# The exponentials stay in the scores' PSUM bank, and the row sums are taken in two parts

## The chip, the core and the metric

The kernel runs on one core of a Trainium2 chip. The metric is the time of one execution in microseconds (us), as the device counts it; less is better. TensorE (PE) multiplies matrices into PSUM, a memory of eight banks of 128 partitions x 512 fp32 values each. VectorE (DVE) and ScalarE (ACT) read and write PSUM and SBUF; GpSimd (POOL) works on SBUF alone here. SyncE (SP) issues the DMAs. Each engine takes its instructions strictly in the order in which they stand in its own queue, and waits on semaphores where it needs another engine's result.

## What is computed

One layer of a bidirectional encoder, on two batches: 256 positions (the prompt) and 2048 positions (the sample), both 1024 wide.

```python
def encoder_layer(x, ...):
    h = rms_norm(x, norm_mix_g)
    q, k, v, x_br, y_br = jnp.split(h @ w_in, splits, axis=-1)
    q, k = rms_norm(q, q_norm_g), rms_norm(k, k_norm_g)   # 8 query heads, 2 key/value heads of 64
    attn = bidir_gqa(apply_axial_rope(q, tables), apply_axial_rope(k, tables), v)
    rec = recurrent_group(x_br, y_br, ...)                # convolution, two gated linear scans
    x = x + jnp.concatenate([attn, rec], axis=-1) @ w_out
    h = rms_norm(x, norm_mlp_g)
    return x + jnp.square(jax.nn.relu(h @ w_up)) @ w_down # 4096 wide

def bidir_gqa(q, k, v):        # per head, no mask
    p = jax.nn.softmax(q @ k.T / 8, axis=-1)
    return p @ v
```

The change touches the softmax and its product with v for the 2048 sample positions.

## The kernel before

**Precision.** Every matmul operand is split into a high part (rounded to the matmul's input type, fp32r, by a copy on ACT) and a low part (the exact value minus the high part, a subtraction on DVE or POOL). A product `w x` is then `wh xh + wh xl + wl xh` (`mm3`, L201 to L204). So nearly every result passes through a cast and a subtraction.

**Stages.** Stage 1 (to about 590 us) projects both batches, normalizes q and k, runs the convolutions and the forward scans, and writes q, k and v as high and low parts to device memory. Stage 2 (L804 on) runs three things beside each other, by generators that are advanced in turn (`tick`): the attention of the sample, in 32 units; the backward scans (`lru_back`, L1157); and the out-projection and MLP of one segment after another (`mlp`, L1091): first the prompt, 256 columns wide, then four segments `s0` to `s3` of 512 columns. A segment of the sample can start only when its eight attention units are done (L1188). `faster(attention(), 5)` gives attention six steps for every five of the MLP. The final order on each engine's queue is set by the recording layer, which schedules with its own model of time; it is fixed when the program is built.

**One attention unit** is one key/value head and 512 queries, so that 8 units make a segment. `guard` (L853) first computes, for the next unit, 16 products of 512 queries with 512 keys (`s_mx`, L867), each reduced on DVE to a maximum (`mx`, L868); the negative maximum becomes a 65th row of the low query operand `ql`. `values` (L956) then walks over 16 chunks of 128 keys. For each chunk:

- L963, L964, PE: two matmuls put the scores less the maximum into a PSUM bank `s` (tag `s`, two banks in pool `pss`).
- L971, ACT: `pf` = exp of the bank, into SBUF (three buffers). From here the bank is free.
- L973, ACT: `ph` = high part of `pf` (three buffers).
- L975, DVE: `pl` = `pf` - `ph`, the low part (three buffers).
- L979 (L977 for the second chunk), POOL: `acc` += `pf`, the running sum that gives the softmax's denominator.
- L967, L968, PE, three chunks later (`LAG`): the value stationary `vv`, 128 columns that hold v's high part and v's low part (64 each), times `ph` and times `pl`, both into the one bank `po`.

`combine` (L904) ends a unit: ACT copies one half of `po` (`sh`, L913), DVE adds the other half to it (`osb`, L914), `acc` is split (L917, L919). After every second unit `finish` (L880) sums `acc` over the partitions by four matmuls into `pden`, takes four reciprocals from it on DVE (L888), multiplies on POOL and stores the result.

**The MLP's PSUM.** The out-projection (`ps_o`), the up-projection (`ps_u`) and the down-projection (`ps_d`) take their banks in turn from `m0`, `m1`, `m2` (L805, `mm_tile`). A tile of `ps_u` is 24 matmuls, one of `ps_d` 12; two `ps_o` tiles are filled together by 48. They are emptied by ACT (L1021, up), by DVE (L1136, `y` += `ps_d`, down) and by DVE (L1003, out-projection). The other banks of stage 2 are two for `s`, two for `aux` (`s_mx`, `pden` and other small uses) and one for `po`: eight in all.

**Others on the engines' queues.** ACT casts the weights (L168); their low parts are taken on DVE or POOL (`wl`, L177), for the prompt's segment two thirds on POOL. DVE makes the MLP's low parts (`ul`, L1025; `h2l`, L1005), and the scans.

Of the kernel before, what the change touches and what calls it, by code (L numbers as in the profile page):

```python
# [12 lines left out]
F32 = mybir.dt.float32  # L13
FR = mybir.dt.float32r
AF = mybir.ActivationFunctionType
ALU = mybir.AluOpType
# [3 lines left out]
P = 128  # L20
D = 1024
KC = D // P
SEQ = 256
DEC = 2048
T = SEQ + DEC
NT = 512
# [25 lines left out]
def f32(ap):  # L52
    return ap.bitcast(F32)
# [23 lines left out]
def trunk(ctx, tc, xT, w_in, w_out, w_up, w_down, vecs, wa, wx, cos, sin, outT):  # L77
    nc = tc.nc
    mm = nc.tensor.matmul
    act = nc.scalar.activation  # L80
    tt = nc.vector.tensor_tensor
    stt = nc.vector.scalar_tensor_tensor
    ts = nc.vector.tensor_scalar
    gtt = nc.gpsimd.tensor_tensor
# [4 lines left out]
    def loadr(out, src):  # L89

        load(f32(out), src)
# [28 lines left out]
    v_d = {r: dtile([P, n // P, 2, P], f"v_d{r}") for r, n in (("p", SEQ), ("s", DEC))}  # L120
# [101 lines left out]
    srcs, saved, scratch = [], [], {}  # L222
    for key in keys:
# [9 lines left out]
        if first:  # L233
# [14 lines left out]
    for i in range(2):  # L248
        o = ctile([P, P], f"ones_{i}", FR)
# [22 lines left out]
    with ExitStack() as c1:  # L272
# [210 lines left out]
        def do_v(r, t0, n, ps):  # L483
            v = sl.tile([P, NT], F32, tag="gy", name="v", bufs=2)
            evac(v[:, :n], ps[:, :n])
            yield
            pt = ps_g.tile([P, NT], F32, tag="g", name="pt")
            for i in range(n // P):
                nc.tensor.transpose(pt[:, i * P:(i + 1) * P], v[:, i * P:(i + 1) * P], ident)
            yield  # L490
            p4 = pt.rearrange("p (i f) -> p i f", f=P)
            for o in range(0, n // P, 2):
                vt = sl.tile([P, NT], FR, tag="xh", name="vt", bufs=2)
                vv = vt.rearrange("p (i k f) -> p i k f", i=2, k=2)
                for kv in range(2):
                    src = p4[:, o:o + 2, 64 * kv:64 * kv + 64]
                    hi = vv[:, :, kv, 64 * kv:64 * kv + 64]
                    act(hi, src, AF.Copy)
                    tt(vv[:, :, kv, 64 - 64 * kv:128 - 64 * kv], src, f32(hi), op=ALU.subtract)
                store(v_d[r][:, t0 // P + o:t0 // P + o + 2], f32(vv))  # L500
                yield

# [299 lines left out]


    with ExitStack() as c2:  # L804
        banks[0] = itertools.cycle(("m0", "m1", "m2"))  # L805
        sm = c2.enter_context(tc.tile_pool(name="m2", bufs=1))
        kvp = c2.enter_context(tc.tile_pool(name="kv", bufs=1))
        qp = c2.enter_context(tc.tile_pool(name="q2", bufs=2))
# [3 lines left out]
        ps_x = c2.enter_context(tc.tile_pool(name="psx", bufs=1, space=PSUM))  # L812

        kv_s = [kvp.tile([P, 2, DEC], FR, tag="k1", name="k1"), kvp.tile([65, 2, DEC], FR, tag="k2", name="k2"),
                kvp.tile([P, DEC // P, 2, P], FR, tag="vv", name="vv2")]
        nc.gpsimd.memset(f32(kv_s[1][64:65]), 1.0)

        def load_kv():
            for o in range(0, DEC, NT):
                load_keys("s", *kv_s[:2], o, NT)  # L820
                yield
            for o in range(0, DEC // P, 4):
                loadr(kv_s[2][:, o:o + 4], v_d["s"][:, o:o + 4])
                yield


# [53 lines left out]
        def finish(u, accs, o_sb):  # L880
# [20 lines left out]
        finals = []  # L901
        pair = []

        def combine(u, po, acc):  # L904
            kv = units[u][2]
            rows = slice(64 * kv, 64 * kv + 64)
            other = slice(64 - 64 * kv, 128 - 64 * kv)
            if kv == 0:
                pair[:] = [sb.tile([P, NT], F32, tag="osb", name="osb", bufs=1), []]
            o_sb, accs = pair  # L910

            sh = sb.tile([P, NT], F32, tag="sh", name="sh", bufs=1)
            act(sh[rows, :], po[other, :], AF.Copy)  # L913
            tt(o_sb[rows, :], po[rows, :], sh[rows, :], op=ALU.add)  # L914
            yield
            ah = sb.tile([P, NT], FR, tag="dh", name="dh", bufs=2)
            act(ah, acc, AF.Copy)  # L917
            al = sb.tile([P, NT], FR, tag="dl", name="dl", bufs=2)
            tt(al, acc, f32(ah), op=ALU.subtract)  # L919
            accs += [(half[kv], ah), (half[kv], al)]  # L920
            yield
            if kv == 1:
                yield from finish(u, accs, o_sb)

        LAG = 3

        def attention():

            tail = []
            qt[0] = load_q(0)  # L930
            yield from guard(0)
            yield
            for u, (kvt, nk, kv, _, _, _) in enumerate(units):
                nkc = nk // P
                k1, k2, vv = kvt
# [4 lines left out]
                tail.append(values(u, po, acc, vv, kv, nkc, qd, ql, k1, k2))  # L940
                i = 0
                while i < nkc or g is not None:
                    i += 1
                    if g is not None and next(g, tail) is tail:
                        g = None
                    for v in list(tail):
                        if next(v, tail) is tail:
                            tail.remove(v)
                    yield
            while tail:  # L950
                for v in list(tail):
                    if next(v, tail) is tail:
                        tail.remove(v)
                yield

        def values(u, po, acc, vv, kv, nkc, qd, ql, k1, k2):  # L956
            p = {}
            pf0 = None
            for c in range(nkc + LAG):
                if c < nkc:  # L960
                    ks = slice(c * P, (c + 1) * P)
                    s = ps_s.tile([P, NT], F32, tag="s", name="s_t")
                    mm(s, k1[:, kv, ks], qd, start=True, stop=False)  # L963
                    mm(s, k2[:, kv, ks], ql, start=False, stop=True)  # L964
                if c >= LAG:
                    ph, pl = p.pop(c - LAG)
                    mm(po, vv[:, c - LAG, kv, :], ph, start=c == LAG, stop=False)  # L967
                    mm(po, vv[:, c - LAG, kv, :], pl, start=False, stop=c == nkc + LAG - 1)  # L968
                if c < nkc:
                    pf = pp.tile([P, NT], F32, tag="pf", name="pf", bufs=3)  # L970
                    act(pf, s, AF.Exp)  # L971
                    ph = pp.tile([P, NT], FR, tag="ph", name="ph", bufs=LAG)
                    act(ph, pf, AF.Copy)  # L973
                    pl = pp.tile([P, NT], FR, tag="pl", name="pl", bufs=LAG)
                    tt(pl, pf, f32(ph), op=ALU.subtract)  # L975
                    if c == 1:
                        gtt(acc, pf0, pf, op=ALU.add)  # L977
                    elif c > 1:
                        gtt(acc, acc, pf, op=ALU.add)  # L979
                    pf0 = pf  # L980
                    p[c] = (ph, pl)
                yield
            yield from combine(u, po, acc)

        def mean_sq(acc, n):
            ps = ps_x.tile([P, NT], F32, tag="aux", name="ps_st", bufs=2)
# [184 lines left out]


        for m in range(KC):
            ws.kept[len(srcs) - KC + m] = [t.rearrange("p a n -> p (a n)" if t is kv_s[0] else "p c a n -> p (c a n)")
                                           [:, NT * m:NT * m + NT] for t in kv_s[::2]]
        spawn(load_kv())
        spawn(faster(attention(), EVERY))
        with ExitStack() as c3:
# [95 lines left out]
```

## Time and profile before

| | |
|---|---|
| runs | 3220.81 us median of three (3219.06 to 3222.16) |
| the profiled execution | 3214.51 us, of which the span from first to last instruction is 3212.4 us |
| PE busy | 3007.6 us (94%) |
| DVE busy | 2066.8 us (64%) |
| ACT busy | 1717.7 us (53%) |
| POOL busy | 1540.9 us (48%) |
| TensorE's granted clock, mean | 0.972 of full speed |

A row of the profile's table of groups, `L975 DVE TENSOR_TENSOR pl<-pf,ph ... x512 | 612.8, 1207 | 168.9 <-ACT ph L973 161.3`, reads: line 975, on DVE, writes `pl` from `pf` and `ph`, 512 times, 612.8 us in all, 1207 ns each; DVE stood idle 168.9 us just before them, of which 161.3 us ended when ACT's `ph` came. A matmul's duration contains its passage through the array, during which the next one already runs; the distance between the starts of two is what a matmul costs.

### The profile page before, as it was taken

How to read it: one execution, taken by the hardware profiler on the slowest of the kernel's cores; microseconds unless marked ns; L12 is line 12 of the kernel's file. 1: busy time of each engine (PE TensorE's matmuls, PEld its weight loads, DVE VectorE, ACT ScalarE, POOL GpSimd, SP SyncE). 2: the span in 40 equal slices, each digit the busy share in tenths (PEclk: the TensorE clock that was granted, in tenths of full speed). 3: DMA queues.
4: the chain of work that ended last, by engine and by line, in shares of the span. 5: the costliest groups of instructions: out<-in, count | busy, mean ns of one | idle time of the engine just before them, and what ended most of it. 6: DMA issues, size and time to landing. Idle time of an engine off the chain costs nothing.

```text
span 3212.4 us, 41900 instructions
## 1 busy us (share of the span) xinstructions
PE 3007.6 (94%) x13646; PEld 2426.9 (76%) x13646; DVE 2066.8 (64%) x2554; ACT 1717.7 (53%) x2956; POOL 1540.9 (48%) x1116
## 2 busy tenths in 40 slices
PE   6699999777899999999999999999999999999998
PEld 5577677556788778888888888888778888778887
DVE  8878876699989986676667766676675311131114
ACT  5475666545566666555556655555566333343334
POOL 4446633567889964453448444443664111321104
PEclk8799999788999999999999999999999999999999
DMA  7656555887665664444447644444664655775554
GB/s 248 209 176 227 159 187 175 258 257 230 197 219 184 222 200 130 140 135 138 142 138 241 196 139 132 146 138 136 206 219 147 193 189 186 254 252 187 189 188 150
DMA packets 342395, 598.97 MB, mean 186 GB/s; under 512 B 44064, under 2 KB 72992, under 8 KB 342176
## 3 DMA queue, kind: packets, MB, share of 16 engines
q1 hardware_dynamic: 342176, 596.30, 57.6%
q8 instruction: 107, 1.75, 0.2%
q14 instruction: 112, 0.92, 0.1%
HBM read 474.52 MB, written 121.63 MB: 186 GB/s over the span
## 4 chain that ended last, share of the span: by engine, by line
PE 64%; DVE 9%; DMA 5%; issue 3%; POOL 3%; ACT 2%; SPq 1%; DVEq 0%; POOLq 0%; ACTq 0%
PE ps_u L204 8%; PE ps_u L202 8%; PE ps_u L203 8%; PE ps_d L204 7%; PE ps_d L203 7%; PE ps_d L202 7%; PE s_t L964 3%; PE s_mx L867 3%; PE s_t L963 3%; PE po L968 3%; PE po L967 3%; DVE pl L975 2%; POOL acc L979 1%; DVE mx L868 1%; PE ps_o L202 1%
## 5 line engine op out<-in xcount | busy, mean ns | idle before, releaser
L168 ACT CAST wh<-wf 128x512 fp32r<-128x512 f32 x712 | 440.3, 619 | 815.1 <-PE ps_d L203 357.2
L979 POOL TENSOR_TENSOR acc<-acc,pf 128x512 f32<-128x512 f32 x448 | 653.3, 1458 | 421.5 <-ACT pf L971 405.3
L975 DVE TENSOR_TENSOR pl<-pf,ph 128x512 fp32r<-128x512 f32 x512 | 612.8, 1207 | 168.9 <-ACT ph L973 161.3
L204 PE MATMUL ps_u<-h2h,wl 128*128 128x512 f32 (+1 forms) x1280 | 480.4, 376 | 9.8 <-POOL wl L177 3.6
L202 PE MATMUL ps_u<-h2h,wh 128*128 128x512 f32 (+1 forms) x1280 | 479.4, 375 | 3.8 <-ACT wh L168 2.0
L203 PE MATMUL ps_u<-h2l,wh 128*128 128x512 f32 (+1 forms) x1280 | 479.3, 375 | 0.7 <-DVE h2l L1005 0.7
L204 PE MATMUL ps_d<-uh,wl 128*128 128x512 f32 (+1 forms) x1248 | 463.7, 374 | 5.3 <-DVE wl L177 4.2
L202 PE MATMUL ps_d<-uh,wh 128*128 128x512 f32 (+1 forms) x1248 | 463.6, 374 | 3.1 <-ACT wh L168 2.2
L203 PE MATMUL ps_d<-ul,wh 128*128 128x512 f32 (+1 forms) x1248 | 463.3, 373 | 0.6 <-DVE ul L1025 0.5
L1023 POOL TENSOR_TENSOR rl<-rl 128x512 f32<-128x512 f32 (+1 forms) x160 | 174.5, 1091 | 601.3 <-ACT uh L1022 590.9
L868 DVE TENSOR_REDUCE mx<-s_mx 128x1 f32<-128x512 f32 x512 | 345.6, 682 | 155.2 <-PE s_mx L867 151.4
L971 ACT ACTIVATE pf<-s_t 128x512 f32<-128x512 f32 x512 | 300.4, 594 | 216.2 <-PE s_t L964 124.1
L1025 DVE TENSOR_TENSOR ul<-rl,uh 128x512 fp32r<-128x512 f32 (+1 forms) x160 | 140.2, 876 | 333.0 <-POOL rl L1023 332.8
L973 ACT ACTIVATE ph<-pf 128x512 fp32r<-128x512 f32 x512 | 317.1, 631 | 11.1 <-PE po L967 2.0
L1136 DVE TENSOR_TENSOR y<-y,ps_d 128x512 f32<-128x512 f32 (+1 forms) x272 | 170.0, 627 | 234.5 <-PE ps_d L204 234.3
L204 PEld LDWEIGHTS ps_u<-h2h,wl 128*128 128x128 f32 x1280 | 243.3, 190 | 62.6 <-POOL wl L177 5.5
L202 PEld LDWEIGHTS ps_u<-h2h,wh 128*128 128x128 f32 x1280 | 243.7, 190 | 53.6 <-ACT wh L168 2.8
L203 PEld LDWEIGHTS ps_u<-h2l,wh 128*128 128x128 f32 x1280 | 243.8, 190 | 49.7 <-DVE h2l L1005 1.1
L204 PEld LDWEIGHTS ps_d<-uh,wl 128*128 128x128 f32 x1248 | 236.7, 190 | 54.9 <-DVE wl L177 6.0
L202 PEld LDWEIGHTS ps_d<-uh,wh 128*128 128x128 f32 x1248 | 236.7, 190 | 52.6 <-ACT wh L168 3.7
L203 PEld LDWEIGHTS ps_d<-ul,wh 128*128 128x128 f32 x1248 | 236.9, 190 | 48.2 <-DVE ul L1025 1.2
L202 PE MATMUL ps_in<-hh,wh 128*128 128x512 f32 (+1 forms) x560 | 221.3, 397 | 40.7 <-DVE wh L168 18.0
(277 smaller groups left out, 5682.3 us busy)
## 6 DMA issues: line engine op xcount, KB each, us to landing
wl<-wl_d SPq DMA_DIRECT2D x624, 256.0 KB, 2.7
wf<-in_w_up_dram SPq DMA_DIRECT2D x320, 256.0 KB, 3.0
wf<-in_w_down_dram SPq DMA_DIRECT2D x320, 256.0 KB, 2.9
wl_d<-wl SPq DMA_DIRECT2D x172, 256.0 KB, 2.9
wf<-in_w_out_dram SPq DMA_DIRECT2D x80, 256.0 KB, 4.0
wh<-wh_d SPq DMA_DIRECT2D x56, 256.0 KB, 3.4
x<-in_xT_dram SPq DMA_DIRECT2D x32, 256.0 KB, 4.9
qd<-q_ds SPq DMA_DIRECT2D x64, 128.0 KB, 3.2
```

The costliest lines, as they stand in the source:

```text
L168: self.copy(i)(tile_, self.f[i])
L202: mm(ps, wh, xh, start=first, stop=False)
L203: mm(ps, wh, xl, start=False, stop=False)
L204: mm(ps, wl, xh, start=False, stop=last)
L868: nc.vector.tensor_reduce(mx[:, i, b:b + 1], s[:, :w], axis=AX.X, op=ALU.max)
L971: act(pf, s, AF.Exp)
L973: act(ph, pf, AF.Copy)
L975: tt(pl, pf, f32(ph), op=ALU.subtract)
L979: gtt(acc, acc, pf, op=ALU.add)
L1023: gtt(e[:, :n], e[:, :n], e[:, :n], op=ALU.mult)
L1025: tt(ul[:, f, :n], e[:, :n], f32(uh[:, f, :n]), op=ALU.subtract)
L1136: tt(y[:, :n], y[:, :n], ps[:, :n], op=ALU.add)
```

## The change

Six edits that belong together:

1. `values`: the exponential is written back into the scores' own bank (`act(s, s, AF.Exp)`); `pf` and its three buffers are gone. `ph` is made from the bank, `pl` is the bank less `ph`. The bank is held until `pl` is done. `ph` has four buffers instead of three.
2. `acc` on POOL sums `ph`, the high parts, instead of the full exponentials.
3. The value stationary in SBUF is 320 columns for each chunk of keys: v's low and high part of head 0, 64 columns of ones, v's high and low part of head 1. `ph` is multiplied with the 128 columns of a head into `po`, as before. `pl` is multiplied with the 128 columns that hold the high part and the ones, into a bank of its own, `pq`: half of `pq` is then the values' sum, the other half the sum of the low parts over the keys, in every partition.
4. `pq` takes the bank `m2` of stage 2; the MLP's tiles take turns on `m0` and `m1` alone.
5. `combine` and `finish`: one copy (`sd`) of `pq`'s sums on ACT and one more addition (`osb` += half of `pq`) on DVE for each unit, and one addition of `pden` and `sd` on DVE for every two units; the reciprocals then read SBUF.
6. `do_v` writes v's two parts in exchanged halves; `load_kv` loads v in eight DMAs of 512-byte pieces instead of four, and POOL fills the ones once.

```diff
@@ do_v
-                    hi = vv[:, :, kv, 64 * kv:64 * kv + 64]
+                    hi = vv[:, :, kv, 64 - 64 * kv:128 - 64 * kv]
@@ stage 2
-        banks[0] = itertools.cycle(("m0", "m1", "m2"))
+        banks[0] = itertools.cycle(("m0", "m1"))
-                kvp.tile([P, DEC // P, 2, P], FR, tag="vv", name="vv2")]
+                kvp.tile([P, DEC // P, 320], FR, tag="vv", name="vv2")]
+        nc.gpsimd.memset(f32(kv_s[2][:, :, 128:192]), 1.0)
@@ load_kv
-                loadr(kv_s[2][:, o:o + 4], v_d["s"][:, o:o + 4])
+                for kv in range(2):
+                    loadr(kv_s[2][:, o:o + 4, 192 * kv:192 * kv + P], v_d["s"][:, o:o + 4, kv])
@@ finish
+            tt(rc, pden, sd, op=ALU.add)
+            yield
             for i in range(4):
-                nc.vector.reciprocal(rc[:, i * P:(i + 1) * P], pden[:, i * P:(i + 1) * P])
+                nc.vector.reciprocal(rc[:, i * P:(i + 1) * P], rc[:, i * P:(i + 1) * P])
@@ combine
             act(sh[rows, :], po[other, :], AF.Copy)
+            act(sd[rows, :], pq[other, :], AF.Copy)
             tt(o_sb[rows, :], po[rows, :], sh[rows, :], op=ALU.add)
+            tt(o_sb[rows, :], pq[rows, :], o_sb[rows, :], op=ALU.add)
@@ attention
                 po = ps_x.tile([P, NT], F32, tag="o", name="po")
+                pq = ps_m.tile([P, NT], F32, tag="m2", name="pq")
@@ values
-                    mm(po, vv[:, c - LAG, kv, :], ph, start=c == LAG, stop=False)
-                    mm(po, vv[:, c - LAG, kv, :], pl, start=False, stop=c == nkc + LAG - 1)
+                    mm(po, vv[:, i, whole:whole + P], ph, start=i == 0, stop=i == nkc - 1)
+                    mm(pq, vv[:, i, part:part + P], pl, start=i == 0, stop=i == nkc - 1)
                 if c < nkc:
-                    pf = pp.tile([P, NT], F32, tag="pf", name="pf", bufs=3)
-                    act(pf, s, AF.Exp)
-                    ph = pp.tile([P, NT], FR, tag="ph", name="ph", bufs=LAG)
-                    act(ph, pf, AF.Copy)
+                    act(s, s, AF.Exp)
+                    ph = pp.tile([P, NT], FR, tag="ph", name="ph", bufs=LAG + 1)
+                    act(ph, s, AF.Copy)
                     pl = pp.tile([P, NT], FR, tag="pl", name="pl", bufs=LAG)
-                    tt(pl, pf, f32(ph), op=ALU.subtract)
+                    tt(pl, s, f32(ph), op=ALU.subtract)
-                        gtt(acc, acc, pf, op=ALU.add)
+                        gtt(acc, acc, f32(ph), op=ALU.add)
```

**Where the order changes.** The first place is PE's queue at the end of the prompt's MLP, where the segment `s0` must wait for its eighth attention unit. `ps_d` is the prompt's last down-projection, `ps_o` the first of `s0`. Before:

```order
L204 MATMUL ps_d<-uh,wl_11037 128x256
L967 MATMUL po<-ph,vv_5227 128x512
L867 MATMUL s_mx<-k_5225,qd 128x512
L968 MATMUL po<-pl,vv_5227 128x512
L867 MATMUL s_mx<-k_5225,qd 128x512 x4
L963 MATMUL s_t<-qd,k_5225 128x512
L964 MATMUL s_t<-ql_10216,k_5226 128x512
L877 MATMUL pm<-ident,m_11267 1x128 x4
L867 MATMUL s_mx<-k_5225,qd 128x512
L202 MATMUL ps_o<-cat_11516,wh_11072 128x512
```

One chunk's score pair stands between the two. After, the same place begins so:

```order
L204 MATMUL ps_d<-uh,wl_10939 128x256
L870 MATMUL s_mx<-k_5225,qd 128x512
L979 MATMUL po<-ph,vv_5227 128x512
L974 MATMUL s_t<-qd,k_5225 128x512
L975 MATMUL s_t<-ql_9545,k_5226 128x512
L980 MATMUL pq<-pl,vv_5227 128x512
L870 MATMUL s_mx<-k_5225,qd 128x512
L979 MATMUL po<-ph,vv_5227 128x512
```

This pattern goes on for 16 score pairs before the first `ps_o` of `s0`, with no MLP matmul among them. 136 pairs stood ahead of the prompt's last down-projection before, and 123 after; 137 and 139 stand ahead of the first `ps_o` of `s0`.

The second place is DVE's queue at the end of an attention unit inside the prompt's MLP. Before:

```order
L975 TENSOR_TENSOR pl<-pf,ph 128x512
L919 TENSOR_TENSOR dl<-acc_9021,dh 128x512
L1025 TENSOR_TENSOR ul<-rl_9578,uh 128x256
L177 TENSOR_TENSOR wl_9636<-wf_9582,wh_9634 128x512
L868 TENSOR_REDUCE mx<-s_mx 128x1
L914 TENSOR_TENSOR osb<-po,sh 64x512
```

After:

```order
L871 TENSOR_REDUCE mx<-s_mx 128x1
L922 TENSOR_TENSOR osb<-po,sh 64x512
L177 TENSOR_TENSOR wl_9107<-wf_9068,wh_9105 128x512
L1146 TENSOR_TENSOR y_5864<-y_5864,ps_d 128x256
L986 TENSOR_TENSOR pl<-s_t,ph 128x512
L923 TENSOR_TENSOR osb<-pq,osb 64x512
```

The subtraction `pl` now reads the scores' bank `s_t`, and the unit's end has a second addition, three instructions behind the first.

## Rows read from the trace of the kernel before

**Rows 1.** The page: busy tenths of the span's 40 slices.

```profile
PE   6699999777899999999999999999999999999998
...
DVE  8878876699989986676667766676675311131114
```

**Rows 2.** Busy time by stretch: window, length, each engine's busy us (instructions), clock, DMA share.

```profile
590.00:1190.00 600.00, 512.88 (x2765) 421.87 (x2766) 552.50 (x635) 352.77 (x657) 477.78 (x338) 0.94 0.69 221
1190.00:2505.00 1315.00, 1311.32 (x5669) 1053.48 (x5668) 898.78 (x1059) 761.28 (x1314) 651.49 (x473) 1.00 0.49 158
2505.00:3212.40 707.40, 688.26 (x3028) 555.29 (x3026) 162.69 (x246) 248.60 (x424) 131.11 (x117) 0.99 0.62 199
```

**Rows 3.** Groups of instructions, 590 to 1190 us, DVE: count, busy us, mean ns.

```profile
L975 DVE TENSOR_TENSOR pl<-pf,ph 128x512 fp32r<-128x512 f32 x162 | 201.9, 1259 | 12.4 <-ACT ph L973 12.4
...
L914 DVE TENSOR_TENSOR osb<-po,sh 64x512 f32<-64x512 f32 x10 | 6.8, 685 | 2.6 <-ACT sh L913 2.5
```

**Rows 4.** Groups by shape, 1190 to 2505 us, DVE: an addition that reads PSUM.

```profile
L1136 DVE TENSOR_TENSOR y<-y,ps_d 128x512 f32<-128x512 f32 x116 | 79.0, 681 | 49.4 <-PE ps_d L204 49.2
```

**Rows 5.** Groups of instructions, 590 to 1190 us, POOL.

```profile
L979 POOL TENSOR_TENSOR acc<-acc,pf 128x512 f32<-128x512 f32 x140 | 221.0, 1578 | 14.9 <-ACT pf L971 11.4
```

**Rows 6.** Groups of instructions, 590 to 1190 us, ACT.

```profile
L973 ACT ACTIVATE ph<-pf 128x512 fp32r<-128x512 f32 x162 | 100.0, 630 | 3.6 <-PE po L967 1.2
...
L971 ACT ACTIVATE pf<-s_t 128x512 f32<-128x512 f32 x162 | 94.3, 592 | 63.6 <-DVE pl L975 20.5 <-PE s_t L964 19.4 <-POOL acc L979 14.9
```

**Rows 7.** Groups by shape, 590 to 1190 us, PE: one of six alike, one of three.

```profile
L204 PE MATMUL ps_u<-h2h,wl 128*128 128x256 f32 x256 | 75.5, 297 | 6.7 <-POOL wl L177 3.6 <-DVE wl L177 3.1
...
L202 PE MATMUL ps_o<-cat,wh 128*128 128x256 f32 x44 | 14.7, 334 | 8.2 <-ACT wh L168 8.2
```

**Rows 8.** Who PE waited for, 590 to 1190 us: total us, times, longest.

```profile
PE po L968 <- DVE pl L975: 33.4, 30, 3.5
```

**Rows 9.** Timeline: start us, duration us, engine, line: one `pl` beside which POOL rested.

```profile
648.84 0.68 DVE L975 TENSOR_TENSOR pl<-pf,ph 128x512 fp32r<-128x512 f32 x1
```

**Rows 10.** Timeline from 1504 us: one chunk, and the bank's next use but one.

```profile
1504.26 0.40 PE L963 MATMUL s_t<-qd,k 128*128 128x512 f32 x1
...
1504.50 0.39 PE L964 MATMUL s_t<-ql,k 65*128 65x512 f32 x1
...
1504.98 0.60 ACT L971 ACTIVATE pf<-s_t 128x512 f32<-128x512 f32 x1 [0.36 <-DVE y L1136]
...
1506.68 1.16 DVE L975 TENSOR_TENSOR pl<-pf,ph 128x512 fp32r<-128x512 f32 x1
...
1509.83 0.39 PE L963 MATMUL s_t<-qd,k 128*128 128x512 f32 x1
```

**Rows 11.** Timeline from 1052 us: one chunk inside the prompt's MLP.

```profile
1052.06 0.39 PE L963 MATMUL s_t<-qd,k 128*128 128x512 f32 x1
...
1055.17 1.14 ACT L973 ACTIVATE ph<-pf 128x512 fp32r<-128x512 f32 x2
```

**Rows 12.** Timeline of DVE from 1056 us: the low part of that chunk.

```profile
1056.79 2.90 DVE L975 TENSOR_TENSOR pl<-pf,ph 128x512 fp32r<-128x512 f32 x2
```

**Rows 13.** Timeline of PE at 859 us: first matmul of the third `ps_d` tile.

```profile
859.57 0.28 PE L202 MATMUL ps_d<-uh,wh 128*128 128x256 f32 x1
```

**Rows 14.** Timeline of DVE at 863 us: the three `ps_d` tiles are added.

```profile
863.25 1.07 DVE L1136 TENSOR_TENSOR y<-y,ps_d 128x256 f32<-128x256 f32 x3
```

**Rows 15.** Timeline of PE at 2368 us: first matmul of one `ps_o` tile.

```profile
2368.18 0.40 PE L202 MATMUL ps_o<-cat,wh 128*128 128x512 f32 x1
```

**Rows 16.** Timeline of DVE to 2375 us: what stood ahead of a `ps_o` tile's addition.

```profile
2368.45 6.15 DVE L1046 SCALAR_TENSOR_TENSOR y<-y,gfin,r 128x512 f32<-128x512 f32 x6
2374.52 0.67 DVE L1003 TENSOR_TENSOR xr<-xr,ps_o 128x512 f32<-128x512 f32 x1
```

**Rows 17.** Busy time by stretch: the start of stage 2, and the prompt's MLP.

```profile
590.00:610.00 20.00, 14.61 (x62) 11.63 (x62) 14.82 (x19) 8.78 (x12) 10.78 (x5) 0.68 1.00 330
...
700.00:1100.00 400.00, 347.95 (x2053) 294.24 (x2053) 384.00 (x437) 244.09 (x462) 342.22 (x239) 0.96 0.64 203
```

More of the change, by code (lines that the diff above doesn't have):

```diff
@@ L878, in guard, with finish @@
             act(ql[64:65, :], pm[0:1, :], AF.Copy, scale=-1.0)
-        def finish(u, accs, o_sb):
+        def finish(u, accs, o_sb, sd):
             _, _, _, _, out, nj = units[u]
@@ L902, in trunk, with combine @@
         pair = []
-        def combine(u, po, acc):
+        def combine(u, po, pq, acc):
             kv = units[u][2]
@@ L908, in combine @@
             if kv == 0:
-                pair[:] = [sb.tile([P, NT], F32, tag="osb", name="osb", bufs=1), []]
-            o_sb, accs = pair
+                pair[:] = [sb.tile([P, NT], F32, tag="osb", name="osb", bufs=1),
+                           sb.tile([P, NT], F32, tag="sd", name="sd", bufs=1), []]
+            o_sb, sd, accs = pair
             sh = sb.tile([P, NT], F32, tag="sh", name="sh", bufs=1)
             act(sh[rows, :], po[other, :], AF.Copy)
+            act(sd[rows, :], pq[other, :], AF.Copy)
             tt(o_sb[rows, :], po[rows, :], sh[rows, :], op=ALU.add)
+            tt(o_sb[rows, :], pq[rows, :], o_sb[rows, :], op=ALU.add)
             yield
@@ L922, in combine @@
             if kv == 1:
-                yield from finish(u, accs, o_sb)
+                yield from finish(u, accs, o_sb, sd)
         LAG = 3
@@ L939, in attention @@
                 po = ps_x.tile([P, NT], F32, tag="o", name="po")
-                tail.append(values(u, po, acc, vv, kv, nkc, qd, ql, k1, k2))
+                pq = ps_m.tile([P, NT], F32, tag="m2", name="pq")
+                tail.append(values(u, po, pq, acc, vv, kv, nkc, qd, ql, k1, k2))
                 i = 0
@@ L954, in attention, with values @@
                 yield
-        def values(u, po, acc, vv, kv, nkc, qd, ql, k1, k2):
+        def values(u, po, pq, acc, vv, kv, nkc, qd, ql, k1, k2):
             p = {}
-            pf0 = None
+            whole, part = 192 * kv, 64 + 64 * kv
             for c in range(nkc + LAG):
@@ L965, in values @@
                 if c >= LAG:
-                    ph, pl = p.pop(c - LAG)
-                    mm(po, vv[:, c - LAG, kv, :], ph, start=c == LAG, stop=False)
-                    mm(po, vv[:, c - LAG, kv, :], pl, start=False, stop=c == nkc + LAG - 1)
+                    i = c - LAG
+                    ph, pl = p.pop(i)
+                    mm(po, vv[:, i, whole:whole + P], ph, start=i == 0, stop=i == nkc - 1)
+                    mm(pq, vv[:, i, part:part + P], pl, start=i == 0, stop=i == nkc - 1)
                 if c < nkc:
-                    pf = pp.tile([P, NT], F32, tag="pf", name="pf", bufs=3)
-                    act(pf, s, AF.Exp)
-                    ph = pp.tile([P, NT], FR, tag="ph", name="ph", bufs=LAG)
-                    act(ph, pf, AF.Copy)
+                    act(s, s, AF.Exp)
+                    ph = pp.tile([P, NT], FR, tag="ph", name="ph", bufs=LAG + 1)
+                    act(ph, s, AF.Copy)
                     pl = pp.tile([P, NT], FR, tag="pl", name="pl", bufs=LAG)
-                    tt(pl, pf, f32(ph), op=ALU.subtract)
+                    tt(pl, s, f32(ph), op=ALU.subtract)
                     if c == 1:
-                        gtt(acc, pf0, pf, op=ALU.add)
+                        gtt(acc, f32(p[0][0]), f32(ph), op=ALU.add)
                     elif c > 1:
-                        gtt(acc, acc, pf, op=ALU.add)
-                    pf0 = pf
+                        gtt(acc, acc, f32(ph), op=ALU.add)
                     p[c] = (ph, pl)
                 yield
-            yield from combine(u, po, acc)
+            yield from combine(u, po, pq, acc)
         def mean_sq(acc, n):
@@ L1173, in trunk @@
         for m in range(KC):
-            ws.kept[len(srcs) - KC + m] = [t.rearrange("p a n -> p (a n)" if t is kv_s[0] else "p c a n -> p (c a n)")
-                                           [:, NT * m:NT * m + NT] for t in kv_s[::2]]
+            ws.kept[len(srcs) - KC + m] = [t.rearrange("p a n -> p (a n)")[:, NT * m:NT * m + NT] for t in kv_s[::2]]
         spawn(load_kv())
```

2 lines of the change are left out of this document (1 added, 1 removed).

## The prediction

> **What bounds the kernel now.** I read the page's slices first, to see where PE has room at all [rows 1]: PE stands at nine tenths from the twelfth slice on, and at seven and eight in the four before it (562 to 883 us), while DVE stands at nine from the ninth to the fourteenth but for one slice. Then I cut the span into stretches and compare each engine's busy time with the length [rows 2]. From 1190 to 2505 us PE is busy 1311 of 1315 us, so no faster VectorE can shorten that part; after 2505 us there is no attention left, and PE has 688 of 707. What can be won lies between 590 and 1190 us, where the prompt's MLP, ten attention units and the backward scans run together. There DVE is busy 552.5 of 600 us, in the 400 us in the middle even 384 [rows 17]. PE's 512.9 us are deceptive, since a matmul's duration contains its passage. In the saturated stretch 5669 matmuls, nearly all 512 wide, take 1315 us, or 0.232 us each [rows 2]. Of the 2765 matmuls between 590 and 1190 us, 6 x 256 + 3 x 44 = 1668 are 256 wide [rows 7], which I take at half, 0.116 us; the other 1097 at most at 0.232. That is at most 448 us of need, so PE loses some 150 us there, and the row of waits names DVE's `pl` first, 33.4 us directly [rows 8]; the rest is spread over weights and tiles that also come late from a full DVE or POOL. POOL has 478 us of 600, ACT 353.
>
> The costliest DVE group there is the low part `pl`: 162 of 1259 ns [rows 3]. The same subtraction took 0.68 us where POOL rested [rows 9]. So what makes it long is POOL beside it, with which it shares something when both of its operands lie in SBUF.
>
> **The change part by part.** Sums go against the profiled execution (3214.5 us, 6.3 us or 0.2% under the median of the runs); I add the 6.3 at the end.
>
> *The subtraction from PSUM.* `pl` takes its first operand from the bank instead of from SBUF. The trace has this kind of operation: `y` += `ps_d`, 512 wide, one operand in PSUM and one in SBUF, took 681 ns on the mean of 116 [rows 4], and `osb`, half of `po` plus an SBUF operand, 685 ns inside the disturbed stretch itself, where POOL is 80% busy [rows 3, 2]. So one operand in PSUM keeps POOL out, and I take 0.681: 162 x (1.259 - 0.681) = -94 us of DVE's work. The bounds are 1.259 (nothing won) and 0.68, and the two rows stand at the lower end. The saturated stretch gets its `pl` shorter too, for nothing: PE is full there.
>
> Those rows show no price for PSUM as such: 0.681 from PSUM, 0.68 from SBUF without POOL. The Trainium skill, "Perfetto Trace Analysis", section "Optimizing Scalar/DVE Operations", states an access overhead of about 60 ns for VectorE on SBUF and 125 ns on PSUM. By that, `pl` would take about 0.745 us, an estimate from that page, and the saving would be 83 us instead of 94; the sum goes by the rows.
>
> *What DVE gets in addition.* A second `osb` for each of ten units, 10 x 0.685 = 6.9, and the addition of `pden` and `sd` for five pairs, 5 x 0.68 = 3.4. DVE's need: 552.5 - 94 + 10 = 469. If the 47 us in which it rests stay, the stretch is 517 us long: **-83 us**. This is close to the others: PE 448, POOL 478 if its operations stay as long as they are. They should get shorter when DVE's `pl` no longer meets them (`acc` takes 1578 ns now [rows 5]), but no row says by how much, and I count nothing for it. In the middle 400 us POOL has 342 and DVE would have about 384 - 62 + 7 = 329 [rows 17]: there POOL is next.
>
> *ACT.* The exponential into PSUM, and the copy `ph` out of PSUM instead of SBUF, are two operations as before, between 0.59 and 0.63 us each whichever of the two rows I take [rows 6]; one more copy `sd` per unit. ACT rests 247 us of the 600: nothing.
>
> *The ones, v's loads.* The ones cost PE no matmul: the `pl` product had 128 columns before and has now. The fill runs once on POOL, which is 10.8 us busy in the first 20 [rows 17]: nothing. v's parts (2048 x 256 x 4 bytes, 2.1 MB) come in pieces half as long, at a time when the DMA engines are 100% busy with 330 GB/s [rows 17], 6.4 us of transfer. Half the rate would cost 6.4 more, the same rate nothing; other loads stand beside, and I take **+2**. `do_v` only exchanges halves: nothing.
>
> *The scores' banks.* A bank is now held until `pl` has read it. In the saturated stretch one chunk ran from 1504.26 to 1506.68 + 1.16 = 1507.84, 3.6 us, and the bank was wanted again at 1509.83 [rows 10]: 2 us to spare, more with a shorter `pl`. In the prompt's MLP another ran from 1052.06 through a late `ph` at 1055.17 [rows 11] to the first of two `pl` that together ran from 1056.79 for 2.90 [rows 12], so to about 1058.2: 6.2 us. Two banks then allow one chunk per 3.1 us; the stretch needs one per 600 / 162 = 3.7 now and per 3.2 if it lasts 517. It just holds; that it doesn't is a rival.
>
> *The stretch of attention alone.* In the new order 16 score pairs stand ahead of `s0`'s first out-projection without an MLP matmul among them. A chunk there is five matmuls, 1.16 us, while the round of two banks is (3.6 - 0.5 for the shorter `pl`) / 2 = 1.55: 16 x 0.39 = **+6** (0 to 10, with the old life).
>
> *Two banks for the MLP.* At 859.57 the third `ps_d` tile began [rows 13]; the first of the three was only added from 863.25 on, three in 1.07 us [rows 14], so until about 863.6. With two banks PE would have waited 4 us in the old order. About eight such groups stand in the prompt's MLP, 32 us at most. But the order is made anew with two banks, and DVE has more air: between 0 and 32 I take half, **+16**. In the samples' segments tiles have 2.8 us and more of matmuls between them, and DVE's addition 0.68: nothing, but for the out-projection. At 2368.18 a `ps_o` tile began [rows 15], while the one two before it had to wait behind six final scalings of 6.15 us and was added at 2374.52 + 0.67 [rows 16]: 7 us. For the three other segments nothing to 7 each; I take 2 together: **+9** (0 to 28).
>
> *The unit's end.* `pq` is one bank; the next unit's first product into it waits for `sd` and the second `osb`, which stands three DVE instructions behind the first. Who waits would be PE, with all behind it. Three instructions of 0.68 are 2.1 us for each of ten units; the product comes three chunks, some 10 us, after the unit's last score, so mostly hidden: of 0 to 20 I take **+5**.
>
> Sum: -83 + 2 + 6 + 16 + 9 + 5 = **-45**: 3169.5 profiled, 3175.8 against the median; I say **3175**.
>
> **Rivals.**
>
> *The two MLP banks eat it.* All groups wait as in the old order: -83 + 2 + 6 + 32 + 28 + 5 = -10, or 3211. For it: `ps_d` tiles of 12 short matmuls come every 1.4 us when PE is alone, and DVE empties them in bunches. Against: DVE falls from 92% to 90% of a shorter stretch, and empties are ordered with the two banks in mind. The Trainium skill, "Perfetto Trace Analysis", section "Optimizing Tensor Performance", bears on this: it advises that independent matmul groups rotate through different PSUM banks, so that one is emptied while the next is filled; here a rotation of three becomes one of two. The row of 859.57 agrees that three are in use.
>
> *More is won.* DVE's idle time shrinks too, because POOL's operations shorten and `pl` no longer queues: DVE 469 plus 20 idle, -111, with some 10 of give-backs: -101, or 3120. For it: PE's need is only 448. Against: POOL at 478.
>
> *The score banks' round binds (slower).* Exp, copy and subtraction are done by two in-order engines that are full of other work; the bank's life includes all of that queueing. Above a life of 2 x 3.7 = 7.4 us the round sets the time, whatever DVE saves: at 8 us, 4.0 us a chunk, 162 x 0.3 = +49, or 3270. Between 6.4 and 7.4 it takes part of the gain: 6.9 would leave 41 of it. For it: the 6.2 us of one chunk. Against: that chunk's `pl` were long ones, and in the rest the exponential came sooner.
>
> *It doesn't do what it says.* `pl` stays at 1.259 us since the bank is also written by ACT, or by other causes: +10 of new DVE work and the +38 of give-backs, 3269. Against: `osb` at 685 ns in the same stretch.
>
> **How the numbers follow.** Forecast 0.59, two MLP banks 0.14, more won 0.14, score banks 0.09, not as said 0.04. The range from 3118 to 3224 takes in the forecast with its bounds, the first rival and the centre of the second, and leaves out half of the latter and both slower ones, 0.20. A measurement here can tell about 0.2% (6.4 us) from no change. Faster: 0.57 of the forecast, 0.14, and half of the first rival, 0.78. Same: 0.02 + 0.06 = 0.08. Slower: 0.09 + 0.04 + 0.01 = 0.14.
>
> **What will show it.** Right: `pl` near 0.68 us everywhere; the start of `s0`'s first out-projection some 60 us earlier; DVE's busy time in the same work down by some 80; the stretch until attention's end still with PE full; PE's waits for `pl` gone, new ones on `ps_d` or `ps_u` for DVE's additions, a few us each. Wrong: score matmuls (L974) waiting for `pl` by tens of us (score banks); MLP matmuls waiting for `y` or `ul` by over 40 us (MLP banks); `pl` over 0.9 us; or a POOL that is full from 700 to 1100 us while DVE rests.

## The result: 17.6 us faster, where 45.8 were forecast

The changed kernel takes 3203.25 us (median of five, 3193.44 to 3204.86), beside 3220.81 us for the kernel before (3218.58 to 3224.41). The ratio is 0.9939, with a 95% interval of 0.9922 to 0.9956. A second measurement, told below, gave 0.9934. So the direction of the forecast was right, and the size was two and a half times too large. The profiled execution has a span of 3203.1 us, 9.3 less than that of before (3212.4); the medians differ by more, so the places below account for the 9.3 and not for all of the 17.6.

Busy time by stretch of the changed kernel, in the columns of [rows 2]: window, length, then PE, weight loads, DVE, ACT and POOL in us (instructions), PE's granted clock, DMA share, GB/s.

```profile
590.00:1190.00 600.00, 528.98 (x2851) 438.66 (x2852) 474.13 (x670) 367.83 (x687) 431.48 (x343) 0.92 0.72 228
1190.00:2505.00 1315.00, 1311.44 (x5669) 1054.27 (x5668) 738.47 (x1077) 757.36 (x1329) 595.85 (x469) 1.00 0.50 158
```

DVE's work fell as the sum had it: 552.5 us between 590 and 1190 us before [rows 2], 474.1 now, 469 forecast. PE's matmuls in the same 600 us rose from 2765 only to 2851. The stretch to 2505 us was full before and is full now, with 160 us of DVE's work gone from it for nothing, as forecast.

The groups of that stretch, 590 to 1190 us, with count, busy us and mean ns, in the changed kernel: DVE's `pl` and the new additions, POOL's `acc`, ACT's two passes.

```profile
L986 DVE TENSOR_TENSOR pl<-s_t,ph 128x512 fp32r<-128x512 f32 x163 | 110.3, 681 | 52.3 <-ACT ph L984 51.8
...
L923 DVE TENSOR_TENSOR osb<-pq,osb 64x512 f32<-64x512 f32 x10 | 6.8, 684 | 1.3 <-ACT sd L921 1.1
...
L890 DVE TENSOR_TENSOR rc<-pden,sd 128x512 f32<-128x512 f32 x5 | 3.4, 683 | 0.0
...
L990 POOL TENSOR_TENSOR acc<-acc,ph 128x512 f32<-128x512 f32 x141 | 194.2, 1378 | 58.7 <-ACT ph L984 55.8 <-DMA r_ds<-rh 1.0
...
L984 ACT ACTIVATE ph<-s_t 128x512 fp32r<-128x512 f32 x164 | 97.1, 596 | 7.8 <-POOL acc L990 2.0
L982 ACT ACTIVATE s_t<-s_t 128x512 f32<-128x512 f32 x164 | 95.3, 583 | 57.8 <-PE s_t L975 55.7 <-DVE mx L871 0.9
```

`pl` went from 1259 [rows 3] to 681 ns, to the nanosecond what the row of `y` had promised. But where DVE stood idle 12.4 us before it, it now stands 52.3 us, waiting for ACT's `ph`: the engine that was the bound now waits.

Who PE waited for in the same stretch: us, times, longest.

```profile
PE s_mx L870 <- DVE mx L871: 21.0, 18, 2.7
PE s_t L974 <- DVE pl L986: 12.4, 11, 2.7
PE po L979 <- ACT ph L984: 11.4, 13, 3.0
```

Of the 33.4 us for `pl` at the product [rows 8], 1.3 are left. In their place stand 12.4 us in which the scores' matmul waits for the bank that `pl` still reads, 11.4 us for `ph`, and 21 for the maxima (18.2 before, in the same view).

The first 610 us from 590 us on, in three parts, before and then changed, in the columns above.

```profile
590.00:800.00 210.00, 158.50 (x733) 122.50 (x734) 195.99 (x218) 106.97 (x204) 148.49 (x105) 0.85 0.80 250
800.00:1050.00 250.00, 224.16 (x1402) 194.71 (x1402) 235.03 (x270) 154.71 (x291) 218.23 (x150) 0.98 0.62 202
1050.00:1200.00 150.00, 140.21 (x676) 112.72 (x675) 131.02 (x159) 98.58 (x176) 118.58 (x90) 0.99 0.65 212
```

```profile
590.00:800.00 210.00, 159.69 (x769) 127.58 (x770) 186.27 (x234) 113.72 (x214) 142.78 (x106) 0.82 0.89 271
800.00:1050.00 250.00, 240.99 (x1577) 214.41 (x1576) 197.30 (x299) 168.32 (x325) 210.85 (x173) 0.99 0.67 221
1050.00:1200.00 150.00, 138.30 (x550) 104.45 (x549) 95.92 (x145) 90.28 (x159) 82.73 (x70) 0.93 0.56 179
```

From the starts of all matmuls I took what PE loses in each part: the time to the next start, less 0.233 us for a 512-wide matmul, 0.117 for one of 256 columns or fewer. Before, the loss is 94.5, 43.2 and 16.8 us, 154.5 in all (the prediction's 150 was right). After, it is 90.5, 19.6 and 25.9 us, 136.0 in all. So the first part gained 4 us, the second 23.6, nearly as much as PE had to give there, and the third lost 9. Outside these parts the two profiles give back some 9 us more: 3 in stage 1, 3 to 4 between 1200 and 2300 us, 7 after 2740 us, less 4 gained between 2300 and 2500 us. The first part shows where the relief of VectorE went: 44 `pl` there are 24 us shorter, yet DVE is still busy 186 of 210 us. The groups of the backward scans take 5 us more there, since these scans moved up (their last `rl` ran at 835.05 before, at 800.89 now), other work fills some 9, and some 10 became rest.

The third part holds the largest single item. PE's timeline around the prompt's end: the last `ps_d` of that phase and the first 512-wide `ps_o` of `s0`, before and then changed.

```profile
1104.51 0.28 PE L204 MATMUL ps_d<-uh,wl 128*128 128x256 f32 x1
...
1109.92 0.47 PE L202 MATMUL ps_o<-cat,wh 128*128 128x512 f32 x1 [0.29 <-DMA cat<-a_ds]
```

```profile
1054.81 0.28 PE L204 MATMUL ps_d<-uh,wl 128*128 128x256 f32 x1
...
1096.84 0.72 PE L202 MATMUL ps_o<-cat,wh 128*128 128x512 f32 x2
```

The prompt's MLP ends 49.7 us sooner, but `s0` begins only 13.1 us sooner. In between, attention runs alone for 42.0 us over 16 score pairs. At five matmuls each these need 16 x 5 x 0.233 = 18.6 us of PE. The forecast allowed 1.55 us for a chunk there; it is 2.6, and from the start of one score pair to the next it is 2.8. The trace has the reason in the banks. From the start of a chunk's score pair to the end of its `pl` (the n-th pair taken with the n-th `pl`) a bank is held 5.3 us on the mean of these 16 chunks, and the pair of the next chunk but one starts 0.3 us later: two banks allow one chunk per 2.8 us. The 5.3 us are 1.4 to the end of the exponential, where the bank came free before the change, and 3.9 from there through `ph` to the end of `pl`.

One piece of that stretch, on ACT and then PE, shows how thin the cover is: ACT loads a function table for the prompt's final normalization (L208) and another for the next exponential (L982), and PE, whose next instruction needs `ph`, waits.

```profile
1087.21 1.28 ACT L208 ACT_TABLE_LOAD   x1
...
1089.00 1.28 ACT L982 ACT_TABLE_LOAD   x1
```

```profile
1091.56 0.79 PE L979 MATMUL po<-ph,vv 128*128 128x512 f32 x1 [2.61 <-ACT ph L984]
1092.15 0.63 PE L870 MATMUL s_mx<-k,qd 128*128 128x512 f32 x1
```

The matmul of 0.63 us is one at the lower of the clock's two levels, 1.2 GHz: from 1087 to 1097 us the granted clock is 0.50. It fell just ahead of this wait; from 1070 to 1086.8 us, still at 1.00, PE had been busy 12.8 of 16.8 us. From 1080 to 1100 us the mean is 0.74.

### The profile page after: what moved, and what is told of

It is laid out like the page before. It is cut to its first block, busy times and chain, and to the rows that moved or that the text cites. A ratio compares the mean times of both kernels' runs of the same rounds, so it can differ in the third digit from the quotient of the medians.

```text
span 3203.1 us, 41975 instructions
## 1 busy us (share of the span) xinstructions
PE 3009.3 (94%) x13646; PEld 2431.3 (76%) x13646; DVE 1823.7 (57%) x2602; ACT 1720.3 (54%) x2988; POOL 1438.2 (45%) x1117
## 4 chain that ended last, share of the span: by engine, by line
PE 68%; DVE 7%; DMA 5%; ACT 3%; issue 2%; POOL 1%; SPq 1%; DVEq 0%; ACTq 0%; POOLq 0%
PE ps_d L204 8%; PE ps_d L202 8%; PE ps_d L203 8%; PE ps_u L204 8%; PE ps_u L203 8%; PE ps_u L202 8%; PE s_t L974 3%; PE s_t L975 3%; PE pq L980 3%; PE po L979 3%; PE s_mx L870 3%; PE ps_o L203 1%; PE ps_o L202 1%; PE ps_o L204 1%; DVE mx L871 1%
## 5 line engine op out<-in xcount | busy, mean ns | idle before, releaser
L990 POOL TENSOR_TENSOR acc<-acc,ph 128x512 f32<-128x512 f32 x448 | 598.8, 1337 | 534.1 <-ACT ph L984 521.6
L986 DVE TENSOR_TENSOR pl<-s_t,ph 128x512 fp32r<-128x512 f32 x512 | 349.6, 684 | 278.6 <-ACT ph L984 274.6
L982 ACT ACTIVATE s_t<-s_t 128x512 f32<-128x512 f32 x512 | 298.1, 583 | 327.5 <-PE s_t L975 310.7
L1033 POOL TENSOR_TENSOR rl<-rl 128x512 f32<-128x512 f32 (+1 forms) x160 | 159.2, 995 | 626.9 <-ACT uh L1032 620.5
L984 ACT ACTIVATE ph<-s_t 128x512 fp32r<-128x512 f32 x512 | 304.7, 597 | 27.7 <-POOL acc L990 2.0
```

What stands on the lines that cost most here:

```text
L982: act(s, s, AF.Exp)
L984: act(ph, s, AF.Copy)
L986: tt(pl, s, f32(ph), op=ALU.subtract)
L990: gtt(acc, acc, f32(ph), op=ALU.add)
L1033: gtt(e[:, :n], e[:, :n], e[:, :n], op=ALU.mult)
```

## The experiments

The ratios are to the kernel before, measured on the same chip, with their 95% intervals.

| run | what differs | us | ratio |
|---|---|---|---|
| e1 | before, MLP on two banks | 3224.89 | 1.0011 (1.0000 to 1.0023) |
| e2 | change, no `pq`, MLP three banks | 3184.35 | 0.9883 (0.9866 to 0.9900) |
| e5 | change, no `pq`, MLP two banks | 3185.93 | 0.9892 (0.9877 to 0.9906) |
| e3 | e5 with a third score bank | 3173.25 | 0.9849 (0.9830 to 0.9869) |
| e8 | e3, the third bank goes to the MLP from `s0` on | 3165.66 | 0.9828 (0.9814 to 0.9843) |
| e4 | change, attention 4 steps to 3 | 3219.08 | 0.9996 (0.9984 to 1.0009) |
| e7 | change, attention 2 steps to 1 | 3326.63 | 1.0330 (1.0314 to 1.0346) |
| e6 | e3 without `pl` | 3163.16 | 0.9814 (0.9798 to 0.9830) |
| e9 | before without `pl` | 3155.15 | 0.9790 (0.9775 to 0.9804) |
| e10 | change, `pq` in `po`'s bank, all its work | 3188.21 | 0.9891 (0.9872 to 0.9909) |
| e11 | change, `pq` in its bank, never read | 3191.30 | 0.9905 (0.9886 to 0.9924) |
| e12 | change, unedited | 3200.24 | 0.9934 (0.9920 to 0.9947) |

### Banks: the MLP's third, and the scores' third

e1:

```diff
-        banks[0] = itertools.cycle(("m0", "m1", "m2"))
+        banks[0] = itertools.cycle(("m0", "m1"))
```

> The kernel before, with the MLP's tiles of stage 2 on m0 and m1 alone (m2 stays empty, nothing else is changed). Theory A, formed from the two traces: the gain was lost to the score banks, which are held until pl has read them, so that attention falls behind the prompt's MLP and runs alone for 16 chunks; the MLP's third bank is worth little: 3215 to 3230 us. Rival B, the third MLP bank is what ate the gain: 3235 to 3253 us.

Measured: 1.0011, some 3.5 us. PE's waits for DVE's `y` and `xr` do appear in its trace, the longest 4.1 us between 590 and 1190 us, but few of them: PE's loss from 590 to 1200 us is 155 us, as before the change.

e2, from the changed kernel:

```diff
-        banks[0] = itertools.cycle(("m0", "m1"))
+        banks[0] = itertools.cycle(("m0", "m1", "m2"))
-                pq = ps_m.tile([P, NT], F32, tag="m2", name="pq")
+                pq = po
-                    mm(pq, vv[:, i, part:part + P], pl, ...)
+                    mm(po, vv[:, i, whole:whole + P], pl, ...)
-            act(sd[rows, :], pq[other, :], AF.Copy)
-            tt(o_sb[rows, :], pq[rows, :], o_sb[rows, :], op=ALU.add)
-            tt(rc, pden, sd, op=ALU.add)
```

> The changed kernel without pq: pl and ph both go into po as before, the MLP keeps its three banks, and no second osb, no sd, no addition to pden is made. The low parts are left out of the softmax's denominator. Two score banks, held until pl has read them, as in the change. In its order 18 score pairs stand alone before s0's first out-projection. Theory A (score banks): the hole stays, 3190 to 3207 us. Rival B (the third MLP bank): 3165 to 3185 us.

Measured: 3184 us, at the edge of what rival B expected, though its order has the hole still (45.4 us without an MLP matmul). Alone it would have spoken for the third MLP bank. The next run, with the same edit but `banks[0]` left at two, corrects that:

> As the run with one po and three MLP banks (no pq, low parts left out of the denominator), but the MLP has two banks and m2 stays empty. Two score banks. It stands between three runs: the changed kernel (it has pq besides), one po with three MLP banks (3184 us), three score banks (3173 us). If pq with its waits, the second osb and the addition to pden cost little, it is near the changed kernel: 3195 to 3206 us, and a free bank is worth 15 to 30 us wherever it goes. If it is pq that costs, 3178 to 3190 us, and the bank is worth little.

Measured: 3186 us. The MLP's third bank is worth 1.6 us here, 0.9892 against 0.9883, which the intervals can't tell apart: with e1, rival B has fallen. What made e2 faster than the change is the absence of `pq` and of its work.

e3, from e5:

```diff
-                    s = ps_s.tile([P, NT], F32, tag="s", name="s_t")
+                    if c % 3 == 2:
+                        s = ps_m.tile([P, NT], F32, tag="m2", name="s_t")
+                    else:
+                        s = ps_s.tile([P, NT], F32, tag="s", name="s_t")
```

> As the run with one po and three MLP banks (low parts left out of the denominator), but the MLP has two banks, and m2 is a third bank for the scores. In its order 3 score pairs stand alone before s0's first out-projection. Theory A (score banks): the hole of some 20 us at 1050 to 1100 us is gone, 3170 to 3190 us. Rival B (the third MLP bank): no better than the changed kernel, 3198 to 3210 us.

Measured: 3173 us, 12.7 less than e5, from which it differs by this edit alone. PE's timeline at the prompt's end:

```profile
1047.49 0.28 PE L204 MATMUL ps_d<-uh,wl 128*128 128x256 f32 x1
...
1061.53 0.65 PE L202 MATMUL ps_o<-cat,wh 128*128 128x512 f32 x1
```

14.0 us lie between the two, in place of 35.7 in e5 and 42.0 in the change. With a third bank the planned order lets attention keep up with the MLP, 137 pairs ahead of the last `ps_d` instead of 127. So the hole came from the score banks, which the change holds longer. e9 below is the other side of it: its two score banks are free after the exponential, as before the change, and its `s0` follows 8.3 us behind the prompt, though the prompt's MLP ends earlier than in the change.

e8 is e3 with m2 as a score bank for the first nine units and an MLP bank after that (`if u < 9 and c % 3 == 2`; `banks[0]` back to three ahead of the loop over `s0` to `s3`).

> The run with three score banks (3173 us), but m2 changes hands: it is the scores' third bank for the first nine attention units, the MLP's third bank from segment s0 on. Low parts left out of the denominator. If the two MLP banks cost only at the out-projections of s0 to s3 (losses after 2740 us: 17 us of PE with two banks, 11 to 13 with three), 3163 to 3171 us; if those are the same with three banks, 3172 to 3177 us.

Measured: 3166 us, 7.6 less than e3. PE's losses after 2740 us fall from 24.3 to 15.5 us, but this says too much: the longest gap, at the first of two out-projections, starts at 2738 us in e8 and at 2740 us in e3, so the edge of the window parts them. Counted from 2500 us on, the loss falls from 25.7 to 21.9 us, and between 1200 and 2500 us from 4.3 to 1.5. This is a version faster than both kernels, at a price in precision: its denominator sums the rounded exponentials.

### Attention ahead in the order

e4 and e7 set `EVERY` from 5 to 3 and to 1.

> The changed kernel with attention advanced four steps for three of the MLP instead of six for five (EVERY 3 instead of 5). In its order 9 score pairs stand alone instead of 16, 140 ahead of the prompt's last down-projection instead of 132. Theory A: about half the hole closes, 3190 to 3200 us. Rival C, the time between 590 and 1100 us is set by something that neither VectorE nor the score banks decide (weights' DMA, the clock): 3200 to 3207 us, the hole's gain is given back ahead of it.

> The changed kernel with attention advanced two steps for each of the MLP (EVERY 1 instead of 5). In its order 142 score pairs stand ahead of the prompt's last down-projection and 5 alone behind it, against 132 and 16 (the run with EVERY 3 in truth had 14 alone). If the hole at the prompt's end is all that is lost, 3183 to 3195 us. If attention's own pace is what lacks (two score banks), the time moves to another place, as with EVERY 3: 3203 to 3225 us.

The order of e4 named there (9 and 140) was not that of this kernel: by its trace 126 pairs stand ahead and 14 alone. In e7's text, too, the counts ahead are too high: by the traces it is 134 in e7 and 124 in the change, where it has 142 and 132. Measured: 3219 us, no better than before the change, and 3327 us, both outside every range expected of them. The time came back elsewhere. In e4 the MLP is absent from PE for 39.4 us at 1045, 24.2 at 1122 and 37.7 at 1773 us; in e7 for 193.8 us at 1103 and 163.8 at 1927. There attention alone starts a unit of 16 chunks every 30.4 us on the mean, 1.9 us a chunk, while PE needs 5 x 0.233 = 1.17 for it. This is the price of attention without cover, and the forecast had 1.55. The banks set it here as well: in these two stretches of e7 a bank is held 3.7 us on the mean and taken again 0.3 us later, which makes 2.0 us a chunk, about the pace measured.

### What is VectorE's relief worth?

e9, from the kernel before; `ph` is used twice:

```diff
-                    pl = pp.tile([P, NT], FR, tag="pl", name="pl", bufs=LAG)
-                    tt(pl, pf, f32(ph), op=ALU.subtract)
-                    p[c] = (ph, pl)
+                    p[c] = (ph, ph)
```

> The kernel before without the low part: pl is not made, both products into po take ph. No bank, no queue and no other operation is changed. VectorE is relieved of 162 x 1.259 = 204 us between 590 and 1190 us, 2.4 times what the change relieves it of. If VectorE's busy time sets the length of that stretch, as the prediction's sum had it, the stretch goes down to PE's need of 448 us: 3065 to 3090 us. Theory E, formed from the runs so far: the relief pays only until PE is full, which it nearly is from 800 us on, and between 590 and 800 us less than half of each us of relief is gained: 3150 to 3180 us.

Measured: 3155 us, inside theory E's range, -68 for 204 us of relief. Since e9 takes `pl` out of the way from the scores to the product as well as out of DVE's queue, not all of the 68 us need be the relief's. Its three parts, in the columns above:

```profile
590.00:800.00 210.00, 170.07 (x854) 134.69 (x855) 178.40 (x210) 121.69 (x234) 164.00 (x117) 0.89 0.88 276
800.00:1050.00 250.00, 239.90 (x1582) 215.11 (x1580) 148.54 (x213) 171.53 (x329) 222.19 (x186) 0.99 0.70 231
1050.00:1200.00 150.00, 149.73 (x640) 119.98 (x639) 62.41 (x89) 97.09 (x172) 76.61 (x62) 0.99 0.58 182
```

From 800 to 1050 us PE runs 1582 matmuls, and in the change 1577: whether DVE is busy 149 or 197 us, PE loses only 16 to 20 us. Before 800 us DVE is still at 178 of 210, and PE loses 73 us, in place of 94.5. Behind 1050 us e9 has no hole like the change's: the prompt's last `ps_d` runs at 1040.52, `s0` begins at 1048.80, and PE loses 3 us there, where the change loses 25.9.

e6 takes `pl` out of e3 in the same way.

> The run with three score banks (3173 us), with the low part left out altogether: pl is not made, and both products into po take ph. VectorE loses another 512 x 0.68 us, some 43 of them between 590 and 800 us, 30 us. Theory D: between 590 and 800 us VectorE still sets the pace (scans, maxima, weights), and the work it was relieved of there was replaced by other work of its own: the loss of PE in that stretch falls by 15 us or more, 3148 to 3163 us. Rival: there the time is set by something else (the loads, the scans' chain through device memory, the clock): 3167 to 3177 us.

Measured: 3163 us, at the edge of theory D's range. PE's loss before 800 us falls from 83.2 to 72.0 us, 11 for the 32 us that `pl` takes there in e3, where 15 were expected. So VectorE sets the pace there in part. What sets the rest was not separated: the granted clock is 0.82 to 0.89 in all these kernels, and if each matmul at the lower level is charged with at most as much again as it needs, the clock accounts for 18 us of the loss in e6 and e9 and 26 in the change at most; the scans' way through device memory and the loads (DMA share 0.89) stay as candidates.

### What `pq` costs

e5 against the change leaves 17 us for `pq`. e10 keeps its work and takes the bank away (`pq = po`); e11 keeps the bank and takes the work away (no `sd`, no second `osb`, no addition to `pden`).

> The changed kernel with pq laid into po's bank: both products add up in the one bank, sd, the second osb and the addition to pden are made as in the change, from that bank (so the output's sums are mixed up). m2 stays empty. It stands between the changed kernel (3203 us) and the run with one po and two MLP banks (3186 us), which has none of that work. If the work at the unit's end costs the 17 us, about 3203 us (3197 to 3209); if it is the second bank and its waits, about 3186 us (3180 to 3192).

> The reverse: the changed kernel with pq in its own bank m2, but sd, the second osb and the addition to pden are left out, so pq is never read (the low parts' share of the values and of the denominator is left out). If the work at the unit's end costs the 17 us, about 3186 us (3180 to 3192); if it is the second bank, about 3203 us (3197 to 3209).

Measured: 0.9891 and 0.9905. Neither alone seems to cost what both do, so neither expectation holds; but the interval of e11 (to 0.9924) meets the change's (from 0.9922). The change was measured again beside them:

> The changed kernel once more, unedited, beside the kernel before, to set the differences of a few us against. The runs with its bank alone (ratio to the kernel before 0.9905) and with its work alone (0.9891) both came out below the change (0.9939). If the two only cost together, the change is at 0.9925 to 0.9950 again, 3198 to 3206 us; if its first measurement lay high and pq costs next to nothing, 0.9890 to 0.9915, 3185 to 3194 us.

Measured: 0.9934. So the cost is real, 0.9892 to 0.9934 or 13 us by this run, and as far as these runs tell it comes when the bank is both held and read. The traces don't show it in a row: PE waits only 1.3 us for `pl` at `pq`. They do show the place. From 590 to 1200 us PE loses 110.5 us in e5, 116 in e2, 120 in e10 and in e11, and 132 to 135 in the two profiles of the change. Each of these kernels also has an order of its own, and e10 has the same 16 pairs alone as the change (41.8 us) and is still faster. What of the 13 us is `pq`'s bank being released later and what is a less lucky order stays open.

## Where the prediction was right and where it failed

- **Where the gain lies, and the subtraction.** Right. The gain lies between 590 and 1190 us, and the full stretch behind it gives nothing; `pl` takes 681 ns; DVE's relief is 201.9 [rows 3] - 110.3 = 92 us, forecast 94; the additions are 6.8 and 3.4 us. The 65 ns that the Trainium skill, "Perfetto Trace Analysis", section "Optimizing Scalar/DVE Operations", would have added for PSUM are not in the row.
- **The step that failed** is "If the 47 us in which it rests stay, the stretch is 517 us long". They did not stay. From 590 to 1200 us DVE's busy time fell by 82.5 us (the three parts above, summed: 562.0 to 479.5), and its rest rose from 48 to 130.5. A busy share of 92% over 600 us was read as one bound over one stretch. The parts differ: ahead of 800 us the relief went to scans, other work and rest, and only 4 us of it to PE; from 800 to 1050 us PE had at most its 43 us to give, of which 24 came; and the end of the stretch is set by attention's eighth unit. Even in e3, with most of the hole closed and without `pq`, PE's loss from 590 to 1200 us is 105 us, 50 less than before, where the term counted 83. e9 shows the same with 204 us of relief: 68 us. The prediction's own figure, PE at 448 of 600, was an average in the same way.
- **Attention alone, +6.** Mis-sized. It is 42.0 us where PE needs 18.6, so 23 us are lost; before, the two rows stand 5.4 us apart in all. The sum took a bank's life, 3.1 us, from the saturated stretch. Alone, it is 3.7 us over the long stretches of e7, a chunk per 1.9 us, and 5.3 here, a chunk per 2.8, with the end of a unit, table loads and a lower clock in it.
- **The score banks.** A rival in the prediction, at 0.09 and as a loss of 49 us. Its mechanism was there, at smaller size: the round of the two banks sets the pace where attention runs alone, there are 12.4 us of direct waits, and the order lets attention fall behind. The third bank gives back 12.7 us.
- **Two MLP banks, +16.** Far too large: 3.5 us in e1, 1.6 between e2 and e5. The advice on rotating banks that the prediction quoted from the Trainium skill ("Perfetto Trace Analysis", "Optimizing Tensor Performance") costs nothing measurable to break in the prompt's MLP, where PE's loss is the same in e1 as before. It has some worth at the out-projections: after 2740 us PE loses 25 us in e1 and 16 before, 23 in e5 and 19 in e2.
- **Out-projections, +9.** Near in sum, wrong in place. At 2368 us nothing was lost; PE's loss between 2300 and 2500 us even fell from 5.7 to 2.0. After 2740 us it rose by 7. Of that the wait for DVE's `xr`, which frees the bank, is less than half: 3.9 us in the change, 1.2 before; the longest gap there, 4.3 us, is a wait for the load of `cat`, 3.3 before.
- **The unit's end, +5.** Too small: `pq` as a whole costs 13 to 17 us, by a way that its waits don't show. The wait that the term priced, PE at `pq` for the second `osb`, is not among PE's waits.
- **v's loads, +2.** Not tried apart. e5 has the same loads as the change.

## What to carry to other kernels

Before a relieved engine's microseconds are turned into time, the stretch has to be cut where the next bound begins: here PE's loss by 50 or 100 us would have shown that from 800 to 1050 us at most 43 us were to be had, and 17 from there to 1200, whatever VectorE did. When two streams must meet (a segment and its eighth attention unit), only the later one's gain counts; ask which of the two a change speeds up. And a buffer that is held longer costs first in the planned order, as lost lead of one stream, long before it shows as a wait on the buffer.

## What the runs showed of the hardware

- POOL's own operations became shorter when DVE's `pl` no longer read both operands from SBUF: `acc` from 1578 [rows 5] to 1378 ns in the prompt's stretch. That `acc` now adds `ph` instead of `pf` is not the reason: in e9, where it still adds `pf` and no `pl` is made, it takes 1413 ns.
- ACT's copy `ph` took 596 ns out of PSUM, 630 [rows 6] out of SBUF, and the exponential 583 into PSUM, 592 [rows 6] into SBUF. The Trainium skill, "Perfetto Trace Analysis", section "Optimizing Scalar/DVE Operations", has ScalarE cheaper on PSUM (about 51 ns of access against 93). The 34 ns of `ph` agree in direction and nearly in size.
